# A hybrid decoder trunk on one core: gates by tanh and a new order of gates, roots and stores in the first part of the in-projection

## The chip, the core and the metric

The kernel runs on one core of one Trainium2 chip. The metric is the device time of one execution in microseconds (us), lower is better. The core has a matrix engine (TensorE, PE in the profile; PEld is its weight load), a vector engine (VectorE, DVE), an engine for activation functions (ScalarE, ACT), GpSimd (POOL) and SyncE (SP). SP's queue issues nearly all transfers here, POOL's some that accumulate.

## What is computed

One layer over 1024 positions of width 1024, in float32:

```python
h = rms_norm(x, g_mix)
z = h @ w_in + b_in              # split: conv value, conv gate, rnn, rnn gate, two merge gates
u = va * sigmoid(ga)             # conformer branch, 1024 channels
y = causal_depthwise_conv(u, w[31]) -> layer_norm -> silu -> @ w_a_out
v = causal_depthwise_conv(xb, w[4])                     # RG-LRU branch, 1536 channels
r = sigmoid(block_diag(v, w_rg_a) + b_a)                # 16 heads of 96
i = sigmoid(block_diag(v, w_rg_x) + b_x)
log_a = -8 * r * softplus(-lam);  a = exp(log_a)
mult = sqrt(-expm1(2 * log_a));   mult[0] = 1
h_t = a_t * h_{t-1} + (mult * i * v)_t                  # a scan over positions
y_b = (h * gelu(gb)) @ w_b_out
x = x + (sigmoid(sa) * y_a + sigmoid(sb) * y_b) @ w_o   # y_a: the conformer branch
x = x + relu(rms_norm(x) @ w_1)**2 @ w_2;  final rms_norm
```

(Names are shortened.) The kernel takes sqrt(1 - a^2) as (a + 1) times the square root of tanh of half of -log_a.

## The kernel before

Products in float32 are made of three products of operands split into a high and a low part, so each 128-column chunk of the in-projection takes 24 pairs of weights and activations times two halves of the positions: 48 matmuls of 512 columns (`chunk_mm`, L729).

The program runs in stages: a start to 54 us, the **first part of the in-projection** (a loop over slots s = 3 to 23, one chunk of `w_in` each, to 351 us), the **second part** (products named z, `zseq`, L926, in which seven products of sub-blocks stand for eight, to about 666 us), then the out-projections and the MLP. The change lies in the first part, and in the first steps of the second.

The order of work in a slot is written out by hand, engine by engine. `CH` gives the chunks' order; slot s processes on the other engines the chunk of slot s - 1. A chunk is of one of three kinds: XB (RG-LRU input: `xb_out` makes xb and its width-4 convolution v, three steps of which run on DVE as `rest`, L486; `xb_parts`, L494, splits v into vth and vtl), GA (conformer gate, `u_gate`, L588) or VA (conformer value, `u_out`). Then `w_parts` splits the weights of the next chunk (L65, L67).

Heads: head n begins at slot 4 + n (one later from head 5 on). `head_mm(n, 0)` and `head_mm(n, 1)` are six 96x96 matmuls each (L534 to L536). Both write the one PSUM buffer "ps2", so each waits until `head_gate` (L542) has read the one before. The first product stands at the end of the head's slot, the second in the next slot behind 18 of the chunk's 24 pairs. The gates' results go by SP transfers (L549) from head rows to 128-channel tiles; they have two buffers, tag "g". `head_load` (L511) brings a head's rows of vth and vtl, `head_w` (L515) its weights.

Scan: for each group of four heads (three tiles of 128 channels) `scan_exp` (L558 exponential, L559 tanh) stands at the end of the slot in `EXP` (8, 13, 17, 21), and `scan_root` (L566, square roots) in the slot after it, ahead of `xb_parts` and of the second gate. `scan_in` multiplies the second gate into v, `scan_tile` (L575 to L578) makes the scan, whose store to `hd` is L579. Sigmoid, exponential with tanh, and square root need different activation tables, which ACT_TABLE_LOAD brings.

DVE's work is collected by `later(ready, cost, ...)` and given out by `vector_work`, in order of the time at which a small model of the engines' clocks has it ready. Steps of the width-31 convolution (`conv`, L640, begun by ScalarE at L622 and L623) fill the gaps that the model sees. The convolution's store is to `yd`. In the last slots `x_load` (L670) and `x_sum` make sums of activations (xs) for the second part, `x_parts` (L686) splits them, and `z_load` (L747) brings weights zw.

SP's order in a slot: weight chunk s + 2 (L60), first gate's transfers, second gate's transfers, head weights, xs loads, stores of scan and convolution, inputs of the next head.

Of the kernel before, what the change touches and what calls it, by code (L numbers as in the profile page):

```python
# [15 lines left out]
P = 128  # L16
# [4 lines left out]
HD = 96  # L21
# [9 lines left out]
def trunk_kernel(ctx: ExitStack, tc: tile.TileContext, x, xt_in, xt_eo, vecs, w_in, w_a_out, w_b_out,  # L31
# [107 lines left out]
    cbw_c = vec[:, 344:392]  # L139
    cbb_c = vec[:, 392:404]  # L140
    lam_c = vec[:, 404:416]
    ba_c = vec[0:HD, 416:432]
    bx_c = vec[0:HD, 432:448]

    xt, xc, raw0 = [], [], []

# [118 lines left out]
    c4 = sm[:, 7, :]  # L265
    csum = cp.tile([P, WA // 2, 8], F32, name="csum")
    cab2 = cp.tile([P, 8], F32, name="cab2")

    def decay():
# [53 lines left out]
        ts_(c8, p_, -8.0, None, ALU.mult)  # L323
        yield
        ts_(c4, p_, 4.0, None, ALU.mult)
        yield

    decaying = decay()
# [6 lines left out]
    with tc.manual_schedule(engines={mybir.EngineType.Activation, mybir.EngineType.DVE,  # L335
# [62 lines left out]
                first_z(i, 1, k, "lh")  # L398
        decay()
        nc.vector.tensor_scalar(cab2, cab_c, 2.0, None, ALU.mult)  # L400
        pairs = caw[:, 8:].rearrange("p (i o j) -> p i o j", o=2, j=8)
        nc.vector.tensor_tensor(csum, pairs[:, :, 0, :], pairs[:, :, 1, :], ALU.add)

# [67 lines left out]
    def xb_out(t, ps):  # L471
# [18 lines left out]
        later(ready, 3.8, rest)  # L490

    def xb_parts(t):
        vp_[t] = T(f"vth{t}", F32R), T(f"vtl{t}", F32R)
        nc.scalar.activation(vp_[t][0], vt[t], AF.Copy)  # L494
        h = vp_[t][0].bitcast(F32)
        later(at("A", 1.06), 1.22, nc.vector.tensor_tensor, vp_[t][1], vt[t], h, ALU.subtract)


    gws = {}
# [18 lines left out]
    def head_w_parts(n):  # L518
# [4 lines left out]
        later(at("A", 0.35), 0.35, nc.vector.tensor_tensor, gl, raw, gh.bitcast(F32), ALU.subtract)  # L523
        gws[n] = (gh, gl)

    gps = {}
# [12 lines left out]
    def head_gate(n, gi, ready):  # L539
        g, hh = divmod(n, 4)  # L540
        a = H(f"g{n}_{gi}", "g")
        nc.scalar.activation(a, gps.pop((n, gi))[:HD, :], AF.Sigmoid,  # L542
                             bias=(ba_c, bx_c)[gi][:, n:n + 1])
        at("A", 1.11, ready)
        for (ti, p0, p1, d0) in PIECES[hh]:
            t = 3 * g + ti
            if (gi, t) not in gate:
                gate[gi, t] = T(f"g{gi}_{t}")
            nc.sync.dma_start(gate[gi, t][p0:p1, :], a[d0:d0 + p1 - p0, :])  # L549

    at_, rooted = {}, {}

    def scan_exp(g):
        at("A", 1.28)
        for t in range(3 * g, 3 * g + 3):
            r = gate[0, t]
            at_[t] = T(f"a{t}")
            nc.scalar.activation(at_[t], r, AF.Exp, scale=c8[:, t:t + 1])  # L558
            nc.scalar.activation(r, r, AF.Tanh, scale=c4[:, t:t + 1])  # L559
            at("A", 2.2)  # L560

    def scan_root(g):
        at("A", 2.56)
        for t in range(3 * g, 3 * g + 3):
            r = gate[0, t]
            nc.scalar.activation(r, r, AF.Sqrt)  # L566
            rooted[t] = at("A", 1.06)

    def scan_in(ready, *ts):
        for t in ts:  # L570
            later(ready, 1.2, nc.vector.tensor_tensor, gate[1, t], gate[1, t], vt.pop(t), ALU.mult)

    def scan_tile(t):
        a, r, i = at_.pop(t), gate.pop((0, t)), gate.pop((1, t))
        nc.vector.scalar_tensor_tensor(r, a, 1.0, r, ALU.add, ALU.mult)  # L575
        nc.vector.memset(r[:, 0:1], 1.0)
        nc.vector.tensor_tensor(i, r, i, ALU.mult)
        nc.vector.tensor_tensor_scan(i, a, i, 0.0, ALU.mult, ALU.add)  # L578
        nc.sync.dma_start(hd[t], i)  # L579

    ut = {}
    yd = dp.tile([8, P, S], F32, name="yd")
# [2 lines left out]
    def u_gate(j, ps):  # L585

        ut[j] = u = T(f"u{j}")
        nc.scalar.activation(u.rearrange("p (o n) -> p o n", o=2), ps.rearrange("p (n o) -> p o n", o=2),  # L588
                             AF.Sigmoid, bias=bin_c[:, GA + j:GA + j + 1])
# [15 lines left out]
    def conv(j):  # L605
# [42 lines left out]
        nc.sync.dma_start(yd[j], acc)  # L648
        yield step()
        if j == 0:  # L650
            ysum.append(T("ysum"))
# [20 lines left out]
    def x_sum(c2):  # L672
        q = xq[c2]
        for n, a, b in ((11, 12, 11), (12, 22, 12), (22, 22, 11), (21, 21, 22)):
            later(0, 1.2, nc.vector.tensor_tensor, q[n], q[a], q[b], ALU.subtract)

    def x_parts(c2, *ps):
        for p in ps:
# [5 lines left out]
                at("A", 2.0)  # L684
            else:
                nc.scalar.activation(h, src, AF.Copy)  # L686
                later(at("A", 1.0), 1.2, nc.vector.tensor_tensor, l, src, h.bitcast(F32),
                      ALU.subtract)

    NU = 6  # L690
    CH = [XB, VA, GA, XB + 1, XB + 2, GA + 1, XB + 3, VA + 1, XB + 4, XB + 5, GA + 2]
# [4 lines left out]
    wraw, wst = {}, {}  # L696
    todo, fresh = [], []

    def later(ready, cost, f, *a):

        todo.append((ready, len(todo), cost, f, a))

    def vector_work(end):
        for ready, _, cost, f, a in sorted(todo, key=lambda x: x[:2]):
            dve(cost, ready, f, *a)
        todo.clear()
        taps["wait"] += fresh
        fresh.clear()
        fill(end)

    def w_load(s):
        if s < NC1:
# [87 lines left out]
    HS0 = [4 + n + int(n > 4) for n in range(NH)]  # L800
    head_at = {s: n for n, s in enumerate(HS0)}

    EXP = {head_slot: g for g, head_slot in enumerate(HS0[4 * g + 3] + 1 for g in range(4))}
# [8 lines left out]
    with tc.manual_schedule(engines=ENGINES):  # L812
        for s in range(3, NC1):
            w_load(s + 2)
            taps["hold"] = s > NC1 - 4
            begun = clk["P"]
            clk["A"], clk["V"] = max(clk["A"], begun + 0.5), max(clk["V"], begun - 2)
# [7 lines left out]
                first_parts(rs)  # L825
                chunk_mm(s, 0, 24, (0,))
            else:
                chunk_mm(s, 0, 18)
            before, new, nxt = (head_at.get(s + d) for d in (-1, 0, 1))
            if before is not None:  # L830

                head_gate(before, 0, begun)
                head_mm(before, 1)
            if s > 3:
                chunk_mm(s, 18, 24)
            if new is not None:
                head_mm(new, 0)

# [7 lines left out]
            elif s > 3:  # L846
                u_out(c - VA, zps[s - 1])
            w_parts(s + 1)
            if s - 1 in EXP:

                scan_root(EXP[s - 1])
            if s == 3 or c >= XB:
                vector_work(0)
                xb_parts(0 if s == 3 else c - XB)
            if before is not None:
                head_gate(before, 1, clk["P"] - 12 * MM)
# [6 lines left out]
            for d in range(5):  # L863
                if s - d in EXP:
                    g = EXP[s - d]
                    if d == 0:
                        scan_exp(g)
                        scan_in(begun + 3.5, 3 * g, 3 * g + 1)
                    elif d == 1:
                        scan_in(begun + 3.5, 3 * g + 2)  # L870

                    t = 3 * g + d - 1
                    if 3 * g <= t < 3 * g + 3 and t < 11:
                        later(rooted[t], 4.8, scan_tile, t)
            if s == NC1 - 1:
                z_get(0, z_lhs)
                z_get(1, z_lhs)
# [8 lines left out]
            vector_work(clk["P"] - 0.7)  # L886
            if nxt is not None:
                head_load(nxt)

# [121 lines left out]
    def z_post2(i, p):  # L1011
# [1131 lines left out]
```

## Time and profile before

| what | before |
|---|---|
| median of 3 runs | 1580.93 us (1578.77 to 1581.06) |
| profiled execution | 1581.38 us, span 1579.6 us, mean granted clock 0.989 |
| PE busy | 1538.3 us (97%) |
| DVE busy | 1232.4 us (78%) |
| ACT busy | 918.4 us (58%) |
| POOL busy | 190.4 us (12%) |
| span 0 to 54 us: PE busy, DMA share | 52.28 us, 0.83 |
| span 666 to 1579.6 us: PE busy, DMA share | 905.30 us of 913.6, 0.65 |

Busy times are those of one profiled execution. A row of a timeline gives start, duration, engine, line, operation, what is written and read, and in brackets the idle time before it with what ended it. A matmul's end is modelled, so starts are read rather than ends.

### The profile page before, as it was taken

To read this page: it belongs to the slowest core of one execution; us is meant where nothing else is said; L and a number is where in the kernel's file an instruction comes from. 1 tells how busy PE (TensorE), PEld (TensorE's weight loads), DVE (VectorE), ACT (ScalarE), POOL (GpSimd) and SP (SyncE) were. 2 spreads that over 40 slices of the span, in tenths; PEclk is the share of its full clock that TensorE was granted. 3 is DMA by queue.
4 is the path that set the end of the run, shared out by engine and by line. 5 is a ranking of instruction groups with operands and counts; after the bars stand their busy time and mean duration, and the time that the engine had idled before them with its cause. 6 is when DMAs were issued, how large, how long until landed. Compare 5 with 4: busy or idle time off the path is not lost.

```text
span 1579.6 us, 19214 instructions
## 1 busy us (share of the span) xinstructions
PE 1538.3 (97%) x6758; PEld 1262.7 (80%) x6758; DVE 1232.4 (78%) x1666; ACT 918.4 (58%) x1290; POOL 190.4 (12%) x225
## 2 busy tenths in 40 slices
PE   9997989898999999999999999999999999999998
PEld 7875767686888888888888888888888888888886
DVE  6996678788899999868596978855555558888897
ACT  6747477476666566724447578644444566555553
POOL 0000000011222222100003233000000001111110
PEclk9999989899999999999999999999999999999999
DMA  8785868698997778964469999533333779889862
GB/s 340 204 195 155 206 153 230 179 277 221 235 259 168 166 187 205 283 233 145 137 181 277 240 193 216 167 129 107 107 120 108 214 238 227 214 221 217 214 134 107
DMA packets 133728, 308.35 MB, mean 195 GB/s; under 512 B 13392, under 2 KB 35408, under 8 KB 133632
## 3 DMA queue, kind: packets, MB, share of 16 engines
q1 hardware_dynamic: 102320, 230.60, 44.9%
q0 software_dynamic: 31168, 76.27, 26.5%
q8 instruction: 53, 0.87, 0.2%
q14 instruction: 43, 0.35, 0.1%
q10 hardware_dynamic: 144, 0.26, 0.0%
HBM read 147.69 MB, written 58.72 MB: 131 GB/s over the span
## 4 chain that ended last, share of the span: by engine, by line
PE 84%; DVE 5%; ACT 4%; issue 4%; DMA 2%; POOL 1%; SPq 0%; POOLq 0%; DVEq 0%; ACTq 0%
PE d L1907 14%; PE yb L1140 8%; PE z L729 7%; PE e L2027 3%; PE keep L1907 2%; PE z L258 2%; DVE y L640 1%; ACT g L542 1%; PE rg L534 1%; ACT a L558 1%; DVE yt L640 1%; PE rg L536 1%; DMA vl<-vtl 1%; DVE v L486 1%; PE rg L535 1%
## 5 line engine op out<-in xcount | busy, mean ns | idle before, releaser
L1919 DVE TENSOR_TENSOR acc<-acc,d 128x1024 f32<-128x1024 f32 x72 | 87.8, 1220 | 33.3 <-PE d L1907 32.7
L729 PE MATMUL z<-xh,win_h 128*128 128x512 f32 x336 | 107.4, 397 | 0.0
L729 PE MATMUL z<-xl,win_h 128*128 128x512 f32 x336 | 106.2, 394 | 0.0
L640 DVE SCALAR_TENSOR_TENSOR y<-u,vec,y 128x511 f32<-128x511 f32 (+14 forms) x120 | 88.4, 737 | 9.0 <-ACT y L622 9.0
L542 ACT ACTIVATE g<-rg,vec 96x1024 f32<-96x1024 f32 x32 | 35.6, 1112 | 90.1 <-PE rg L536 51.2
L729 PE MATMUL z<-xh,win_l 128*128 128x512 f32 x336 | 83.0, 391 | 0.0
L640 DVE SCALAR_TENSOR_TENSOR yt<-u,vec,yt 128x511 f32<-128x511 f32 (+6 forms) x112 | 82.6, 737 | 0.0
L640 DVE SCALAR_TENSOR_TENSOR y<-yt,csum,y 128x511 f32<-128x511 f32 (+6 forms) x112 | 82.6, 737 | 0.0
L729 PEld LDWEIGHTS z<-xh,win_h 128*128 128x128 f32 x336 | 64.7, 193 | 15.0 <-ACT win_h L67 0.7
L729 PEld LDWEIGHTS z<-xl,win_h 128*128 128x128 f32 x336 | 64.2, 191 | 13.9
L729 PEld LDWEIGHTS z<-xh,win_l 128*128 128x128 f32 x336 | 63.1, 188 | 14.4
L66 POOL DMA_DIRECT2D zo<-zw x48 | 42.0, 874 | 157.1 <-ACT zo L65 142.4
L1581 ACT ACTIVATE o<-s 128x512 fp32r<-128x512 f32 x56 | 33.8, 624 | 45.7 <-DVE s L1565 26.4
L486 DVE SCALAR_TENSOR_TENSOR v<-xb,vec,v 128x1023 f32<-128x1023 f32 (+2 forms) x36 | 46.2, 1283 | 13.6 <-ACT v L477 12.6
L66 POOL DMA_DIRECT2D win_l<-win_raw x21 | 18.3, 873 | 317.5 <-ACT win_l L65 274.7
L1140 PE MATMUL yb<-hgl,wb_h 128*128 128x512 f32 x168 | 51.7, 389 | 0.0
L1140 PE MATMUL yb<-hgh,wb_h 128*128 128x512 f32 x168 | 51.7, 389 | 0.0
L534 PE MATMUL rg<-vh,rgh 96*96 96x512 f32 x64 | 27.1, 424 | 21.2 <-ACT g L542 15.9
L65 ACT ACTIVATE zo<-zw 128x512 fp32r<-128x512 f32 x48 | 30.0, 625 | 23.6 <-issue 4.2
L66 POOL DMA_DIRECT2D db_1l<-wr x7 | 6.1, 872 | 310.7 <-ACT db_1l L65 288.1
L1140 PE MATMUL yb<-hgh,wb_l 128*128 128x512 f32 x168 | 41.0, 389 | 0.0
L1104 DVE TENSOR_TENSOR o<-s,o 128x512 fp32r<-128x512 f32 x56 | 37.3, 684 | 1.5 <-ACT o L1581 1.4
(1872 smaller groups left out, 4801.3 us busy)
## 6 DMA issues: line engine op xcount, KB each, us to landing
w_raw<-in_w_dram SPq DMA_DIRECT2D x34, 512.0 KB, 5.4
fr<-fd SPq DMA_DIRECT2D x32, 512.0 KB, 5.7
wr<-in_w_dram SPq DMA_DIRECT2D x32, 512.0 KB, 6.5
zw<-in_w_in_dram SPq DMA_DIRECT2D x28, 512.0 KB, 6.2
zo<-zw POOLq DMA_DIRECT2D x48, 256.0 KB, 5.3
win_raw<-in_w_in_dram SPq DMA_DIRECT2D x21, 512.0 KB, 7.7
win_l<-win_raw POOLq DMA_DIRECT2D x21, 512.0 KB, 7.9
zo<-zs POOLq DMA_DIRECT2D x32, 256.0 KB, 6.1
```

Source lines behind the costliest of these rows:

```text
L66: nc.gpsimd.dma_start(l, src, accum_op=ALU.add)
L486: nc.vector.scalar_tensor_tensor(v[:, d:S], a[:, 0:S - d], cbw_c[:, w * 12 + t:w * 12 + t + 1], v[:, d:S], ALU.mult, ALU.add)
L534: nc.tensor.matmul(o, gh[:, gi, :], vh[:, hs], start=True, stop=False)
L542: nc.scalar.activation(a, gps.pop((n, gi))[:HD, :], AF.Sigmoid, bias=(ba_c, bx_c)[gi][:, n:n + 1])
L640: nc.vector.scalar_tensor_tensor(o[:, k:], a[:, 0:HS - k], c, o[:, k:], ALU.mult, add)
L729: nc.tensor.matmul(zps[s][:, HALVES[hf]], w[:, k, :], xw[k][part][hf], start=n == 0, stop=n == 23)
L1104: tt(l, src, h.bitcast(F32), ALU.subtract)
L1140: nc.tensor.matmul(ps[hf], a, b[:, HALVES[hf]], start=n == 0, stop=n == len(todo) - 1)
L1581: nc.scalar.activation(o[:, 0], src, AF.Copy)
L1907: nc.tensor.matmul(o, a, b, start=n == 0 and (p != 1 or g == 0), stop=n == len(todo) - 1, skip_group_check=p == 1 and g > 0)
L1919: tt(acc[p, q2], acc[p, q2], ps, ALU.add)
L2027: nc.tensor.matmul(o, a, b, start=n == 0 and t not in LOADED, stop=n == len(todo) - 1, skip_group_check=t in LOADED)
```

## The change

Seven things are changed together.

- Gates: sigmoid(x) becomes tanh(x / 2), whose factor and summand are folded into what follows: constants of the exponential and tanh (`c8`, `c4`), halved biases (`bhalf`), the root's scale of 0.25, the first column's 0.5, `scan_in` as (gate + 1) * v, and in `u_out` a ScalarE Identity that halves the value in PSUM (one for each of six conformer chunks).
- `scan_exp` of a group's first tile moves one slot earlier; that of the other two stays in the slot of before, behind the second gate.
- `scan_root` moves to the end of its slot, behind the second gate.
- `put` and `flush_puts`: in the first part the second gate's transfers and the stores of scan and convolution are held and issued at the start of the next slot, behind the weight chunk's load. The first gate's transfers are issued at once.
- DVE's work has three ranks (`soon`, `later`, `idle`); `urgent` gives out only rank 0 ahead of `xb_parts`, and the scan's three parts are separate items.
- The second head product stands behind 15 of 24 pairs instead of 18.
- In the second part `x_parts(0, 4)` and `x_parts(1, 4)` move from its steps 0 and 4 to 3 and 5.

```diff
-        nc.scalar.activation(a, gps.pop((n, gi))[:HD, :], AF.Sigmoid,
-                             bias=(ba_c, bx_c)[gi][:, n:n + 1])
+        nc.scalar.activation(a, gps.pop((n, gi))[:HD, :], AF.Tanh, scale=0.5,
+                             bias=bax_h[gi][:, n:n + 1])
...
-            nc.sync.dma_start(gate[gi, t][p0:p1, :], a[d0:d0 + p1 - p0, :])
+            put(gate[gi, t][p0:p1, :], a[d0:d0 + p1 - p0, :], gi == 0)
...
-    def scan_exp(g):
-        at("A", 1.28)
+    def scan_exp(*ts):
+        for t in ts:
+            r = gate[0, t]
+            at_[t] = T(f"a{t}")
+            c = c8[:, t:t + 1], c4[:, t:t + 1]
+            nc.scalar.activation(at_[t], r, AF.Exp, scale=c[0], bias=c[0])
+            nc.scalar.activation(r, r, AF.Tanh, scale=c[1], bias=c[1])
+            at("A", 2.2)
+
+    def scan_root(g):
+        at("A", 1.28)
         for t in range(3 * g, 3 * g + 3):
             r = gate[0, t]
-            at_[t] = T(f"a{t}")
-            nc.scalar.activation(at_[t], r, AF.Exp, scale=c8[:, t:t + 1])
-            nc.scalar.activation(r, r, AF.Tanh, scale=c4[:, t:t + 1])
-            at("A", 2.2)
...
-            nc.scalar.activation(r, r, AF.Sqrt)
+            nc.scalar.activation(r, r, AF.Sqrt, scale=0.25)
             rooted[t] = at("A", 1.06)
+        at("A", 1.28)
...
-            later(ready, 1.2, nc.vector.tensor_tensor, gate[1, t], gate[1, t], vt.pop(t), ALU.mult)
+            idle(ready, 1.28, nc.vector.scalar_tensor_tensor, gate[1, t], gate[1, t], 1.0, vt.pop(t),
+                 ALU.add, ALU.mult)
...
-        later(clk["A"], 1.28, nc.vector.scalar_tensor_tensor, uv,
-              ps.rearrange("p (n o) -> p o n", o=2), bin_c[:, VA + j:VA + j + 1], uv,
-              ALU.add, ALU.mult)
+        nc.scalar.activation(ps, ps, AF.Identity, scale=0.5, bias=bva_h[:, j:j + 1])
+        later(at("A", 1.11), 1.28, nc.vector.scalar_tensor_tensor, uv, uv, 1.0,
+              ps.rearrange("p (n o) -> p o n", o=2), ALU.add, ALU.mult)
...
+    def put(o, i, now=False):
+
+        if now or part[0] > 1:
+            nc.sync.dma_start(o, i)
+        else:
+            held_puts.append((o, i))
...
             w_load(s + 2)
+            flush_puts()
...
-                chunk_mm(s, 0, 18)
+                chunk_mm(s, 0, 15)
...
-            if s - 1 in EXP:
-
-                scan_root(EXP[s - 1])
             if s == 3 or c >= XB:
-                vector_work(0)
+                urgent()
                 xb_parts(0 if s == 3 else c - XB)
...
+            for g, e in EXP.items():
+                if s == e - 1:
+                    scan_exp(3 * g)
+                elif s == e:
+                    scan_exp(3 * g + 1, 3 * g + 2)
+                    scan_in(begun + 3.5, 3 * g, 3 * g + 1)
+                elif s == e + 1:
+                    scan_in(begun + 3.5, 3 * g + 2)
+                    scan_root(g)
+                t = 3 * g + s - e - 1
+                if e < s and t < min(3 * g + 3, 11):
+                    scan_tile(t)
...
-    ZX = {0: ((x_parts, 0, 4), (x_parts, 1, 6)), 1: ((x_parts, 1, 7),), 2: ((x_parts, 1, 5),),
-          4: ((x_parts, 1, 4),), 7: ((later, 0, 4.8, scan_tile, 11),)}
+    ZX = {0: ((x_parts, 1, 6),), 1: ((x_parts, 1, 7),), 2: ((x_parts, 1, 5),),
+          3: ((x_parts, 0, 4),), 5: ((x_parts, 1, 4),), 7: ((scan_tile, 11),)}
```

More of the change, by code (lines that the diff above doesn't have):

```diff
@@ L400, in trunk_kernel @@
         nc.vector.tensor_scalar(cab2, cab_c, 2.0, None, ALU.mult)
+        nc.vector.tensor_scalar(bhalf[:, 0:16], bin_c[:, 0:16], 0.5, None, ALU.mult)
+        nc.vector.tensor_scalar(bhalf[:, 16:48], vec[:, 416:448], 0.5, None, ALU.mult)
         pairs = caw[:, 8:].rearrange("p (i o j) -> p i o j", o=2, j=8)
@@ L488, in rest @@
                                                ALU.mult, ALU.add)
-        later(ready, 3.8, rest)
+        soon(ready, 3.9, rest)
     def xb_parts(t):
@@ L495, in xb_parts @@
         h = vp_[t][0].bitcast(F32)
-        later(at("A", 1.06), 1.22, nc.vector.tensor_tensor, vp_[t][1], vt[t], h, ALU.subtract)
+        soon(at("A", 1.06), 1.22, nc.vector.tensor_tensor, vp_[t][1], vt[t], h, ALU.subtract)
     gws = {}
@@ L522, in head_w_parts @@
         nc.scalar.activation(gh, raw, AF.Copy)
-        later(at("A", 0.35), 0.35, nc.vector.tensor_tensor, gl, raw, gh.bitcast(F32), ALU.subtract)
+        soon(at("A", 0.35), 0.35, nc.vector.tensor_tensor, gl, raw, gh.bitcast(F32), ALU.subtract)
         gws[n] = (gh, gl)
@@ L556, in scan_exp, with start, scan @@
             r = gate[0, t]
-            at_[t] = T(f"a{t}")
-            nc.scalar.activation(at_[t], r, AF.Exp, scale=c8[:, t:t + 1])
-            nc.scalar.activation(r, r, AF.Tanh, scale=c4[:, t:t + 1])
-            at("A", 2.2)
[L562 to L566, printed above, removed]
+            nc.scalar.activation(r, r, AF.Sqrt, scale=0.25)
             rooted[t] = at("A", 1.06)
+        at("A", 1.28)
     def scan_in(ready, *ts):
         for t in ts:
-            later(ready, 1.2, nc.vector.tensor_tensor, gate[1, t], gate[1, t], vt.pop(t), ALU.mult)
+            idle(ready, 1.28, nc.vector.scalar_tensor_tensor, gate[1, t], gate[1, t], 1.0, vt.pop(t),
+                 ALU.add, ALU.mult)
     def scan_tile(t):
         a, r, i = at_.pop(t), gate.pop((0, t)), gate.pop((1, t))
[L575 to L579, printed above, removed]
+        ready = rooted[t]
+        def start():
+            nc.vector.scalar_tensor_tensor(r, a, 1.0, r, ALU.add, ALU.mult)
+            nc.vector.memset(r[:, 0:1], 0.5)
+        def scan():
+            nc.vector.tensor_tensor_scan(i, a, i, 0.0, ALU.mult, ALU.add)
+            put(hd[t], i)
+        idle(ready, 1.35, start)
+        idle(ready, 1.22, nc.vector.tensor_tensor, i, r, i, ALU.mult)
+        idle(ready, 2.3, scan)
     ut = {}
@@ L588, in u_gate @@
         nc.scalar.activation(u.rearrange("p (o n) -> p o n", o=2), ps.rearrange("p (n o) -> p o n", o=2),
-                             AF.Sigmoid, bias=bin_c[:, GA + j:GA + j + 1])
+                             AF.Tanh, scale=0.5, bias=bga_h[:, j:j + 1])
         at("A", 1.11)
@@ L674, in x_sum @@
         for n, a, b in ((11, 12, 11), (12, 22, 12), (22, 22, 11), (21, 21, 22)):
-            later(0, 1.2, nc.vector.tensor_tensor, q[n], q[a], q[b], ALU.subtract)
+            soon(0, 1.2, nc.vector.tensor_tensor, q[n], q[a], q[b], ALU.subtract)
     def x_parts(c2, *ps):
@@ L686, in x_parts @@
                 nc.scalar.activation(h, src, AF.Copy)
-                later(at("A", 1.0), 1.2, nc.vector.tensor_tensor, l, src, h.bitcast(F32),
-                      ALU.subtract)
+                soon(at("A", 1.0), 1.2, nc.vector.tensor_tensor, l, src, h.bitcast(F32),
+                     ALU.subtract)
     NU = 6
@@ L697, in trunk_kernel, with later, soon, idle @@
     todo, fresh = [], []
-    def later(ready, cost, f, *a):
-        todo.append((ready, len(todo), cost, f, a))
+    counter = [0]
+    def later(ready, cost, f, *a, rank=1):
+        counter[0] += 1
+        todo.append((rank, ready, counter[0], cost, f, a))
+    def soon(*a):
+        later(*a, rank=0)
+    def idle(*a):
+        later(*a, rank=2)
+    def work(items):
+        while items:
+            x = min((x for x in items if x[1] <= clk["V"]), default=None) or min(items, key=lambda x: x[1:3])
+            items.remove(x)
+            _, ready, _, cost, f, a = x
+            dve(cost, ready, f, *a)
+    def urgent():
+        first = [x for x in todo if x[0] == 0]
+        todo[:] = [x for x in todo if x[0]]
+        work(first)
     def vector_work(end):
-        for ready, _, cost, f, a in sorted(todo, key=lambda x: x[:2]):
-            dve(cost, ready, f, *a)
+        items = todo[:]
         todo.clear()
+        work(items)
         taps["wait"] += fresh
@@ L709, in vector_work, with flush_puts @@
         fill(end)
+    held_puts = []
+    part = [1]
+    def put(o, i, now=False):
[3 more added lines that the diff above has]
+            held_puts.append((o, i))
+    def flush_puts():
+        for o, i in held_puts:
+            nc.sync.dma_start(o, i)
+        held_puts.clear()
     def w_load(s):
@@ L801, in trunk_kernel @@
     head_at = {s: n for n, s in enumerate(HS0)}
-    EXP = {head_slot: g for g, head_slot in enumerate(HS0[4 * g + 3] + 1 for g in range(4))}
+    EXP = {g: HS0[4 * g + 3] + 1 for g in range(4)}
     XS = {NC1 - 4: ((x_load, 0),), NC1 - 3: ((x_sum, 0),), NC1 - 2: ((x_load, 1), (x_parts, 0, 6)),
@@ L862, in trunk_kernel @@
                 head_w(head_at[s + 2])
[L863 to L874, printed above, removed]
+            for g, e in EXP.items():
[10 more added lines that the diff above has]
+                    scan_tile(t)
             if s == NC1 - 1:
@@ L888, in trunk_kernel @@
                 head_load(nxt)
+        flush_puts()
+        part[0] = 2
     stage.close()
```

15 lines of the change are left out of this document (8 added, 7 removed).

## The prediction

> **What bounds the kernel now.** I read the page first. Its span and busy parts say that TensorE is the bound, and that little of it is free:
>
> ```profile
> span 1579.6 us, 19214 instructions
> PE 1538.3 (97%) x6758; PEld 1262.7 (80%) x6758; DVE 1232.4 (78%) x1666; ACT 918.4 (58%) x1290; POOL 190.4 (12%) x225
> ```
>
> So the question is where the 41 us that PE lacks lie, and at which clock it runs beside them. The windows view, cut by stage, answers that (columns: length, busy us and count of PE, weight loads, DVE, ACT, POOL; granted clock, DMA share, GB/s):
>
> ```profile
> 54.00:66.41 12.41, 12.41 (x55) 10.05 (x56) 11.11 (x13) 8.09 (x10) 1.02 (x2) 1.00 0.94 217
> 66.41:351.06 284.65, 259.36 (x1099) 205.31 (x1098) 223.36 (x286) 177.13 (x180) 17.64 (x21) 0.95 0.77 198
> 351.06:370.42 19.36, 13.42 (x51) 10.33 (x50) 19.28 (x22) 12.12 (x18) 4.14 (x5) 0.91 0.83 204
> 213.60:226.00 12.40, 5.11 (x13) 3.76 (x13) 12.10 (x14) 9.65 (x11) 0.00 (x0) 0.59 0.55 143
> 366.00:660.00 294.00, 293.91 (x1290) 243.24 (x1291) 268.57 (x402) 191.30 (x325) 65.70 (x75) 0.99 0.82 209
> ```
>
> Slots 5 to 23 of the first part (66.41 to 351.06) leave PE idle for 284.65 - 259.36 = 25.3 us at a mean clock of 0.95; the first 19.4 us of the second part leave 5.9 us at 0.91. From there to 660 PE is full at 0.99. The waits view from 60 to 370 us names the waits (total, times, longest):
>
> ```profile
> PE rg L534 <- ACT g L542: 15.9, 4, 7.3
> PE rg L534 <- DMA vh<-vth: 5.3, 1, 5.3
> PE rg L536 <- DMA vl<-vtl: 4.1, 1, 4.1
> PE z0a L926 <- ACT z0b L992: 3.1, 1, 3.1
> PE z1a L926 <- ACT z1b L992: 2.8, 1, 2.8
> ```
>
> The first three are head products. A head's two products share one PSUM buffer, so each waits until ScalarE's gate (L542) has emptied it. The PE timeline shows a slot without a stall and the worst wait:
>
> ```profile
> 172.26 0.40 PE L534 MATMUL rg<-vh,rgh 96*96 96x512 f32 x1
> 172.96 0.39 PE L534 MATMUL rg<-vh,rgh 96*96 96x512 f32 x1
> 186.00 0.40 PE L534 MATMUL rg<-vh,rgh 96*96 96x512 f32 x1
> 220.92 0.74 PE L534 MATMUL rg<-vh,rgh 96*96 96x512 f32 x1 [7.29 <-ACT g L542]
> ```
>
> A slot with two head products takes 186.00 - 172.26 = 13.74 us. Three head matmuls take 172.96 - 172.26 = 0.70, so a product takes 1.40, a slot with one 12.34, one with none 10.94. A chunk's 48 matmuls thus go at 0.228 us each.
>
> What ScalarE did ahead of 220.92 (its timeline in slot 14):
>
> ```profile
> 205.49 1.15 ACT L559 ACTIVATE g<-g,sm 128x1024 f32<-128x1024 f32 x1
> 206.66 1.28 ACT L542 ACT_TABLE_LOAD   x1
> 207.95 1.11 ACT L542 ACTIVATE g<-rg,vec 96x1024 f32<-96x1024 f32 x1
> 208.97 1.10 ACT L474 ACTIVATE xb<-z,vec 128x1024 f32<-128x1024 f32 x1
> 210.10 1.25 ACT L477 ACTIVATE v<-xb,vec 128x1024 f32<-128x1024 f32 x1
> 211.25 1.04 ACT L65 ACTIVATE win_l<-win_raw 128x1024 fp32r<-128x1024 f32 x1
> 212.20 1.04 ACT L67 ACTIVATE win_h<-win_raw 128x1024 fp32r<-128x1024 f32 x1
> 213.25 1.28 ACT L566 ACT_TABLE_LOAD   x1
> 214.54 2.95 ACT L566 ACTIVATE g<-g 128x1024 f32<-128x1024 f32 x3
> 217.40 1.04 ACT L494 ACTIVATE vth<-v 128x1024 fp32r<-128x1024 f32 x1
> 218.46 1.28 ACT L542 ACT_TABLE_LOAD   x1
> 219.75 1.11 ACT L542 ACTIVATE g<-rg,vec 96x1024 f32<-96x1024 f32 x1
> ```
>
> Between the splits and the second gate (219.75) stand two table loads and three square roots: 1.28 + 2.95 + 1.28 = 5.5 us. The first gate too was late, behind six exponential and tanh instructions and a load. The first part has 15 loads, by the view that groups lines:
>
> ```profile
> L542 ACT ACT_TABLE_LOAD x6 | 7.7, 1283 | 0.1
> L558 ACT ACT_TABLE_LOAD x4 | 5.1, 1283 | 0.1
> ```
>
> (the roots' four at L566, of which 213.25 is one, and one at L588 make the 15). The DMA waits come from elsewhere, shown by SyncE's queue:
>
> ```profile
> 131.25 12.34 SPq L549 DMA_DIRECT2D g<-g  x2
> 144.31 0.72 SPq L579 DMA_DIRECT2D hd<-g  x1
> 145.12 0.54 SPq L511 DMA_DIRECT2D vh<-vth  x1
> ```
>
> The second gate's transfers held the queue for 12.34 us until the late gate was there; a store of the scan followed, and only then the inputs of the next head.
>
> **Part 1: table sets, roots and exponentials.** Sigmoid becomes tanh(x/2), with the factors folded into neighbours. Exponential and tanh already run in turn without a load (one load at L558 for six instructions in each of four groups). So the loads in front of the exponentials and of the next gate go, and 4 x 2 remain around the roots: 15 - 8 = 7 loads, 9.0 us of ScalarE. Against that stand six new Identity instructions in `u_out`, at the 1.10 of L474 each: 6.6 us. ScalarE's sum is nearly unchanged; what matters is the order. I walk a slot with time 0 at its chunk's first matmul. PE now: 30 matmuls to 6.8, the second product to 8.2, 18 matmuls to 12.3, the next head's first product to 13.7. The first gate must end by 6.8, the second by 12.3. ScalarE in a value slot: gate 1.1, xb 2.2, v 3.4, two splits 5.5. The three DVE steps of the width-4 convolution follow v:
>
> ```profile
> L486 DVE SCALAR_TENSOR_TENSOR v<-xb,vec,v 128x1023 f32<-128x1023 f32 (+2 forms) x36 | 46.2, 1283 | 13.6 <-ACT v L477 12.6
> ```
>
> 3 x 1.28 = 3.85, so vth runs at 7.3 to 8.4 and the second gate ends at 9.5: 2.8 before it is needed. Of six exponentials and tanhs (1.15 each) two now stand in the slot before and four behind the second gate: they end 14.5, 0.8 into the next slot. That is the root slot: first gate to 1.95, second to 10.4 (slack 1.9), head weights 0.35, load and roots 4.2: 15.1, 1.4 into the next slot. There, load and first gate end at 3.9 against 6.8; slots 15, 19 and 23 work on gate and value chunks of the conformer branch and have no vth, and slot 10 has no gate. No wait is left by this sum. What is late next is the second gate of slots 14 and 18, by 1.9 us of slack.
>
> **Part 2: the queue.** Second gates' transfers and the scan and convolution stores go at the start of the next slot, behind the load of a weight chunk. Head inputs are queued at a slot's end with nothing late ahead; they have some 11 us until use. New is that a scan's store may wait for DVE ahead of the first gate's transfers and the head weights: by the walk in slots 10 and 11, up to 6 us into the slot; the inputs queued behind still have over half a slot. The 5.3 and 4.1 us go.
>
> **Sum for slots 5 to 23.** Ideal: 14 x 13.74 + 3 x 12.34 + 2 x 10.94 = 251.3. Measured 284.65. Gain 33.4, of which 25.3 is idle time and 8.1 slow matmuls behind it: the row 213.60 to 226.00 shows 13 matmul records in 5.1 us at clock 0.59.
>
> **Part 3: the start of the second part.** The rows are of DVE's, ScalarE's and SP's timelines, the fourth of the chain of waits:
>
> ```profile
> 322.06 5.08 DVE L462 TENSOR_TENSOR xs<-xs,xs 128x1024 f32<-128x1024 f32 x4 [9.07 <-issue]
> 364.50 1.06 ACT L686 ACTIVATE xs7h<-xs 128x1024 fp32r<-128x1024 f32 x1 [3.79 <-DVE g L578]
> 366.09 4.49 PE z1a L926 x12
> 315.36 2.04 SPq L670 DMA_DIRECT2D xs<-xu  x4
> ```
>
> DVE stood 9.07 us for xs, whose loads left SP at 315.36, late in the slot, behind a second gate's transfers. From there it ran without a pause, and ScalarE's copies z0b and z1b were late behind it. After the change the loads leave behind the first gate instead, DVE gets those 9 us back, and four `x_parts` subtractions and a scan are ordered behind what z needs first. z0b must end 5.9 us into z and by this sum ends about 2 us earlier. At the pitch of 366 to 660, 293.91 / 1290 = 0.228 us, the 51 matmuls take 11.6 of the 19.36 us: 7.7 gained. The last chain row has the clock's part in it: 12 matmuls in 4.49. [...]
>
> **Costs.** In slot 3 `u_out` stands ahead of the split of the next chunk, for which PE then waits:
>
> ```profile
> 52.86 1.05 ACT L67 ACTIVATE win_h<-win_raw 128x1024 fp32r<-128x1024 f32 x1
> ```
>
> The split ends at 53.91 and the chunk starts at once, so the new Identity costs up to its 1.1 and at least 0: I take 1.0. The other five lie in slots without vth and are covered by 2.7 us and more. Two tiny DVE steps in the start: 0. Residual waits: between 0 and the 9.4 us of DMA waits; I take 2.5, near the low end, since the slack in the walk is never under 1.9. In the second part a move of DVE work (about 4 us of convolution) into a stage where it is busy 268.57 of 294: 25 us of room, 0.
>
> Sum: 33.4 + 7.7 - 1.0 - 2.5 = 37.6. The profiled execution took 1581.38 us (span 1579.6 and 1.8 around it), the median of the runs is 1580.93, 0.45 less: 1580.93 - 37.6 = 1543.3.
>
> **The rivals.** (a) *The start of z keeps its stall*, since DVE's queue into z is full either way: 7.7 back, 1551. For it: DVE has no pause from 322 to 370. Against: the 9.07 us ahead. (b) *Transfers become the bound.* 0.77 x 284.65 = 219 us of DMA time now fits into 254: a share of 0.86. One late head input as at 146 to 157 costs 5.3 + 4.1 and some 2.5 of slow matmuls: 1555. Against: 54.00 to 66.41 ran at a share of 0.94 with PE full. (c) *Other ScalarE waits*: a late DVE uses up the 1.9 us of slack in the root slots, and half of the 15.9 stays, with 2.5 of slow matmuls twice: 1556. Against: DVE is busy 223.36 of 284.65, and the convolution's steps now give way to what is urgent. (d) *The tables still switch at each group*, tanh sharing no set with exp: against it the rows L558 and L559, in turn without loads. The 7 loads would stay on ScalarE, at worst all on the path: 1543 + 9.0 = 1552. (e) *Slower*: held transfers of second gates. Gate outputs have two buffers, so a second gate waits until the last one's transfer, now issued some 2 us into the slot, has landed. From a landing later than 12.3 - 1.1 = 11.2 us into the slot each of 14 slots loses the excess; 37.6 / 14 = 2.7, so from 13.9 on the gain is gone, and at 14.5 it is 1543 + 14 x 3.3 = 1589. The DMA view shows such transfers landing in 4 to 5 us:
>
> ```profile
> g<-g SPq DMA_DIRECT2D x16, 384.0 KB, 4.3
> ```
>
> That puts the landing near 7: unlikely, but queues of the moved stores run before it.
>
> **How the numbers follow.** Forecast (1538 to 1548) 0.60; (a) 0.10; (b) 0.12; (c) 0.07; (d) 0.02; (e) or another loss 0.06; a null 0.03. What a measurement can tell from no change is 0.2%, about 3.2 us. Faster: 0.60 + 0.10 + 0.12 + 0.07 + 0.02 = 0.91. The range goes from 1538 (no residual, no Identity cost, 1543.3 - 3.5 = 1539.8, and 1.8 for the reading of the slot length) to 1558, past (a) to (d).
>
> **What would show it.** Right: table loads in the first part 8; slots of 13.7, 12.3 and 10.9 us throughout, clock 0.98 or more; no PE wait over 1 us on L542's successor; head inputs landing before 9 us into their slot; z's first 51 matmuls in under 13 us. Wrong: waits of rg on the gate with ScalarE idle and a gate buffer's DMA as its releaser (e), on vh (b), of z0a on z0b (a), or on a gate with ScalarE busy (c).

## The result and the profile after

The changed kernel takes 1551.15 us, the median of 5 runs (1550.6 to 1555.04), against 1580.93 us; ratio 0.9819, 95% interval 0.9803 to 0.9835. That is 29.8 us faster. 37.6 us were forecast (1543.3), the range was 1538 to 1558.

The page of the changed kernel, and its waits of PE from 50 to 360 us (total, times, longest):

```profile
span 1553.3 us, 19218 instructions
PE 1532.6 (99%) x6758; PEld 1258.8 (81%) x6758; DVE 1231.3 (79%) x1668; ACT 915.5 (59%) x1289; POOL 190.1 (12%) x225
...
PE rg L537 <- ACT g L545: 5.8, 3, 4.9
PE z1b L975 <- DMA zo<-zs: 2.8, 1, 2.8
PE z L778 <- ACT win_h L67: 1.0, 1, 1.0
PE z0a L975 <- ACT z0b L1041: 1.0, 1, 1.0
```

The profiled execution is the slowest of the five (1555.04 us). A second profile of the same kernel, *again* below, took 1551.85 us, which is nearer to the median. So I read both. The windows view for slots 5 to 23 and for the head of the second part (from its first matmul to the first with xs4, 125 matmuls by the view), first the head of before (its slots stand in the prediction), then of the changed kernel, then of *again*:

```profile
351.06:387.22 36.16, 30.22 (x125) 24.22 (x124) 32.47 (x38) 23.40 (x37) 7.66 (x9) 0.95 0.81 203
```

```profile
67.29:326.56 259.27, 253.46 (x1099) 202.07 (x1098) 225.37 (x286) 175.02 (x181) 19.09 (x22) 0.99 0.85 219
326.56:360.68 34.12, 30.31 (x125) 24.26 (x124) 31.36 (x38) 21.87 (x34) 6.20 (x8) 0.95 0.82 200
```

```profile
67.59:320.91 253.32, 251.81 (x1100) 201.00 (x1098) 224.08 (x285) 173.47 (x178) 18.26 (x21) 1.00 0.86 223
320.91:356.12 35.21, 30.06 (x126) 24.16 (x125) 32.60 (x39) 23.13 (x37) 7.00 (x8) 0.95 0.83 200
```

The slots went from 284.65 to 259.27 us, and to 253.32 in *again*, where the ideal of the prediction was 251.3. The head of the second part went from 36.16 to 34.12 and 35.21: in sum most of its stall is still there, though not in the same place, as is shown below. The slot before (4) ends 0.9 to 1.2 us later. In *again* the account is 31.3 us gained in the slots and 1.0 in the head, less 1.2 at slot 4, 1.1 in the rest of the second part and 0.5 behind it: 29.5, its span being 1550.1.

### The profile page after: what moved, and what is told of

Same layout as the page of the kernel before. It is cut to its first block, busy times and chain, and to the rows that moved or that the text cites. A ratio compares the mean times of both kernels' runs of the same rounds, so it can differ in the third digit from the quotient of the medians.

```text
span 1553.3 us, 19218 instructions
## 1 busy us (share of the span) xinstructions
PE 1532.6 (99%) x6758; PEld 1258.8 (81%) x6758; DVE 1231.3 (79%) x1668; ACT 915.5 (59%) x1289; POOL 190.1 (12%) x225
## 4 chain that ended last, share of the span: by engine, by line
PE 83%; DMA 5%; issue 5%; DVE 4%; POOL 1%; ACT 1%; SPq 0%; POOLq 0%; DVEq 0%; ACTq 0%
PE d L1956 15%; PE z L778 9%; PE yb L1189 8%; PE e L2076 3%; PE keep L1956 2%; DMA g<-g 2%; DMA xs<-xu 1%; PE z L256 1%; PE rg L537 1%; PE rg L538 1%; PE rg L539 1%; DMA x<-in_x_dram 1%; DVE v L489 1%; POOL go L66 1%; DVE g L465 1%
## 5 line engine op out<-in xcount | busy, mean ns | idle before, releaser
L1968 DVE TENSOR_TENSOR acc<-acc,d 128x1024 f32<-128x1024 f32 x72 | 87.8, 1219 | 33.4 <-PE d L1956 32.7
L545 ACT ACTIVATE g<-rg,bhalf 96x1024 f32<-96x1024 f32 x32 | 35.4, 1107 | 51.0 <-PE rg L539 33.1
L66 POOL DMA_DIRECT2D win_l<-win_raw x21 | 18.3, 873 | 289.3 <-ACT win_l L65 225.2
L1189 PEld LDWEIGHTS yb<-hgh,wb_h 128*128 128x128 f32 x168 | 31.5, 188 | 6.6
```

What stands on the lines that cost most here:

```text
L66: nc.gpsimd.dma_start(l, src, accum_op=ALU.add)
L545: nc.scalar.activation(a, gps.pop((n, gi))[:HD, :], AF.Tanh, scale=0.5, bias=bax_h[gi][:, n:n + 1])
L1189: nc.tensor.matmul(ps[hf], a, b[:, HALVES[hf]], start=n == 0, stop=n == len(todo) - 1)
L1968: tt(acc[p, q2], acc[p, q2], ps, ALU.add)
```

## The experiments

The runs fall into four groups: the control, parts of the change taken back, parts put into the kernel before, and other orders at the head of the second part. Times are medians of the timed runs. The kernel before ran at 1580.7 to 1581.6 beside them.

**The control**, the changed kernel itself.

> The changed kernel itself, as a control and for a second profile. The profiled execution on record took 1555.0 us, the median 1551.2. Theory one (the waits of the gate in slot 18 and of z1b for zo both belong to the program): both show again, each within 1 us, and the run is at 1550 to 1555. Theory two (one of them comes and goes with the landing of transfers): one of them is absent in this profile, and the profile's time is nearer 1551.

It took 1551.27 us, ratio 0.9807 (0.9794 to 0.982). Its PE waits:

```profile
PE z1b L975 <- DMA zo<-zs: 2.8, 1, 2.8
PE z0a L975 <- ACT z0b L1041: 2.3, 1, 2.3
PE rg L537 <- ACT g L545: 1.4, 2, 0.9
```

Theory two holds for the gate of slot 18: its 4.9 us wait is absent here. The wait of z1b shows in both. In the profile on record DVE had stood for a tile that a held store of the scan was still reading:

```profile
236.25 1.66 SPq L757 DMA_DIRECT2D hd<-g  x1
...
245.53 1.23 DVE L465 TENSOR_TENSOR vtl<-v,vth 128x1024 fp32r<-128x1024 f32 x1 [6.00 <-DMA hd<-g]
...
259.83 1.06 ACT L497 ACTIVATE vth<-v 128x1024 fp32r<-128x1024 f32 x1 [5.03 <-DVE v L489]
...
261.94 0.67 PE L537 MATMUL rg<-vh,rgh 96*96 96x512 f32 x1 [4.87 <-ACT g L545]
```

The chain is store, tile, DVE (which then works without a pause until the split can start), split, gate, PE. The store landed 9.2 us after its issue, in *again* 5.4. Two other profiles with this order, of *xs4_in_gap* and *scan_behind_sums* below, have the pair again: DVE waits 5.4 and 5.3 us for the store, PE 4.3 and 4.2 us for the gate. What makes the landing differ between executions stays open.

**Stores at once.**

```diff
-            put(hd[t], i)
+            put(hd[t], i, True)
-        put(yd[j], acc)
+        put(yd[j], acc, True)
```

> Only the stores of scan and convolution are issued at once again; second gates' transfers stay held. Theory (a held store keeps a tile from DVE, which stood 6.0 us for vtl's buffer, and the late DVE held the gate of slot 18 for 4.9 us and some 2.4 us of slow matmuls): DVE's wait and PE's wait go, 1544 to 1548 us. Rival (the stores belong behind the head inputs): PE waits for vh or vl, 1553 to 1560 us.

It took 1577.51 us, ratio 0.998 (0.9972 to 0.9989): 26.2 us of the gain were gone. The theory was wrong. The rival had the direction and a small part: PE waited 4.5 us for vh once, in slot 10, which took 18.3 us instead of 12.3. Its gate waits weigh more, 20.4 us in all: slots 15 and 19 took 25.0 and 25.3 us instead of 13.7. Its timelines of SP, then of ScalarE and PE in slot 15, and its waits of ScalarE and of SP:

```profile
215.32 0.33 SPq L751 DMA_DIRECT2D hd<-g  x1
215.74 0.51 SPq L514 DMA_DIRECT2D vh<-vth  x1
...
220.01 1.37 SPq L60 DMA_DIRECT2D win_raw<-in_w_in_dram  x1
221.48 1.79 SPq L757 DMA_DIRECT2D g<-g  x1
```

```profile
230.17 1.11 ACT L545 ACTIVATE g<-rg,bhalf 96x1024 f32<-96x1024 f32 x1 [12.84 <-DMA g<-g]
231.33 0.74 PE L537 MATMUL rg<-vh,rgh 96*96 96x512 f32 x1 [9.83 <-ACT g L545]
```

```profile
ACT g L545 <- DMA g<-g: 38.7, 6, 13.1
SPq L751 <- DVE g L587: 65.0, 6, 15.8
```

The store waits in SP's queue for the scan, which the change has put last on DVE. All behind it waits too, and the held transfer of the second gate leaves only at 221.48. The gate's buffer is free 8.7 us later, and the next second gate stood 12.84 us for it, PE 9.83. This is the mechanism of the prediction's rival (e), the loss through the two gate buffers, with a place and a price. That the stores stand behind the head inputs is what keeps the change from it.

**Second gates at once**, stores held.

```diff
-            put(gate[gi, t][p0:p1, :], a[d0:d0 + p1 - p0, :], gi == 0)
+            put(gate[gi, t][p0:p1, :], a[d0:d0 + p1 - p0, :], True)
```

> Second gates' transfers are issued at once, stores of scan and convolution stay held. Theory (what blocks the queue is a transfer that waits for a late DVE or ScalarE; the second gate now ends near 9.5 us into the slot and is not late): head inputs leave at 10 us instead of earlier, about even, 1549 to 1554 us, and the gates' waits for their own buffers' transfers (11.8 us in the profile of the change) shrink. Rival (holding the second gates is what pays): head inputs late behind them, PE waits for vh, 1560 to 1572 us.

It took 1553.62 us, ratio 0.9829 (0.9815 to 0.9844), within the theory; the interval overlaps the control's. Of the held transfers the stores matter here, the second gates little.

**Roots ahead** of vth and the second gate.

```diff
+            for g, e in EXP.items():
+                if s == e + 1:
+                    scan_root(g)
             if s == 3 or c >= XB:
                 urgent()
...
-                    scan_root(g)
```

> Only the square roots go back ahead of vth and the second gate; tanh gates, spread exponentials and held transfers stay. Theory (the roots' place is the main part of the gain): in a root slot the second gate ends 5.5 us later, 15.9 instead of 10.4 us into the slot against 12.3, so 3.6 us and some 2.4 us of slow matmuls in each of two to four slots: 1563 to 1575 us. Rival (seven table loads fewer and the early exponential give enough room): under 5 us, 1551 to 1556.

It took 1549.9 us, ratio 0.9802 (0.9789 to 0.9816): no loss, as the rival had it, and a little under its span. ScalarE's timeline in slot 14 of this kernel:

```profile
193.60 1.04 ACT L67 ACTIVATE win_h<-win_raw 128x1024 fp32r<-128x1024 f32 x1
194.65 1.28 ACT L569 ACT_TABLE_LOAD   x1
195.94 2.96 ACT L569 ACTIVATE g<-g 128x1024 f32<-128x1024 f32 x3
198.81 1.04 ACT L497 ACTIVATE vth<-v 128x1024 fp32r<-128x1024 f32 x1
```

DVE ends the convolution that vth needs at about 197.5 (three steps in 3.91 us from 193.62). So load and roots fill 2.9 us in which ScalarE would wait anyway, and vth is 1.3 us late, not 5.5. The second gate, behind one more load, starts 12.85 us into this slot, against 12.29 in *again*.

**Sigmoid gates**, and sigmoid with roots ahead. The first undoes the diff's lines on tanh, constants, `scan_in` and the Identity; the second adds the edit above.

> Gates by sigmoid again, with the constants of before and without the six Identity instructions; the order of roots and exponentials, the ranks, the held transfers and the 15 pairs stay. Theory (the queue's order is the main part, table loads only take slack that ScalarE has in most slots): 7 loads of 1.28 us come back, one of them ahead of a first gate and one ahead of exponentials in each group; PE waits for gates by 3 to 8 us in all, 1552 to 1560 us. Rival (the tables are the main part): the gate waits of before, 15.9 us with their slow matmuls, are back: 1570 to 1577 us.

> Sigmoid gates as in sigmoid_back (1555.3 us), and the square roots also back ahead of vth and the second gate; held transfers, ranks, spread exponentials and the 15 pairs stay. Theory (tables and the roots' place back each other up: with tanh only one load stands between roots and second gate, and with roots last the extra loads fall behind the second gate, so each alone is nearly free): both taken away give back gate waits of 3 to 7 us with slow matmuls in two or three slots, 1564 to 1575 us. Rival (the roots' place does not matter at all, as the run with roots ahead and tanh gates says): 1553 to 1558 us.

They took 1555.32 us (ratio 0.984, 0.9826 to 0.9855) and 1557.59 us (0.9852, 0.9839 to 0.9866). The first is within the theory's span: the tables are worth 4.1 us of the time. The count in the theory was off: with the exponentials spread over two slots I count 23 loads in the first part for sigmoid gates, 15 more than the changed kernel's 8 and not 7. That is an estimate from the order of ScalarE's work and the places of the 15 loads of before; it was not shown. For the second the rival's time was right. Its two gate waits of 6.0 and 4.9 us are there as the theory said, and its slots are 6.6 us longer than those of *sigmoid_back*, but PE waits less in the second part. The net is 2.3 us, and the two intervals overlap:

```profile
PE rg L537 <- ACT g L545: 10.9, 2, 6.0
PE z1b L976 <- DMA zo<-zs: 0.8, 1, 0.8
PE z2a L976 <- DMA zo<-zw: 0.7, 1, 0.7
```

**Exponentials in one slot.**

```diff
-                if s == e - 1:
-                    scan_exp(3 * g)
-                elif s == e:
-                    scan_exp(3 * g + 1, 3 * g + 2)
+                if s == e:
+                    scan_exp(3 * g, 3 * g + 1, 3 * g + 2)
```

> The changed kernel with a group's six exponential and tanh instructions in one slot, behind the second gate. Theory (the root slot has 1.9 us of slack by the prediction's walk, and two more instructions take 2.4): waits of 0.5 to 2 us in two or three slots, 1551 to 1556 us. Rival (the spread is a main part): waits of 3 us and more with slow matmuls, 1560 to 1570 us.

It took 1556.32 us, ratio 0.9842 (0.9829 to 0.9856): 5.0 us over the control, 0.3 above the theory's span. Its gate waits are 3.0 and 0.7 us; a wait of 5.4 us for z0b was in neither account. By its profile 5.4 us are lost in the slots against *again* and 2.6 in the head of the second part, and 2.1 come back elsewhere.

**The kernel before with transfers held**, and with roots last as well.

```diff
             w_load(s + 2)
+            flush_puts()
...
-            nc.sync.dma_start(gate[gi, t][p0:p1, :], a[d0:d0 + p1 - p0, :])
+            put(gate[gi, t][p0:p1, :], a[d0:d0 + p1 - p0, :], gi == 0)
...
-        nc.sync.dma_start(hd[t], i)
+        put(hd[t], i)
```

(`yd` likewise, and `put` and `flush_puts` as in the change; in the second kernel `scan_root(g)` moves behind the second gate.)

> The kernel before with one thing of the change: second gates' transfers and the stores of scan and convolution are held to the start of the next slot. Theory (queue order alone removes the waits for vh and vl, 9.4 us with some 2.5 of slow matmuls, and xs comes earlier; the four gate waits of 15.9 us stay): 1564 to 1571 us. Rival (the gate buffers come free later, and gates that are late already get later): no gain or slower, 1578 to 1590 us.

> The kernel before with two things of the change: held transfers and stores (1570.9 us alone), and the square roots behind the second gate. Theory (its two waits of 7.4 and 7.3 us are the roots and loads ahead of the second gate): they go with their slow matmuls, some 2 x 10 us less 2 to 4 that the later first gates lose: 1552 to 1558 us. Rival (loads and roots only move on to the next slot's first gate, and the exponentials in one slot are what is missing): 1564 to 1571 us.

They took 1570.87 us (ratio 0.9943, 0.9927 to 0.996) and 1567.72 us (0.9913, 0.9899 to 0.9926). The queue alone gains 9.8 us, in the theory's span; by its profile 7.5 us come in the slots and 3.1 in the head of the second part. It keeps the gate waits, and one short wait for vl:

```profile
PE rg L534 <- ACT g L542: 18.2, 7, 7.4
...
PE rg L536 <- DMA vl<-vtl: 1.3, 1, 1.3
```

Roots last adds only 3.2 us, the rival's case. Its two long gate waits are 4.0 and 3.9 us in place of 7.4 and 7.3. Its slots gain 5.2 us, and the head gives 2.6 back: z0a waits 5.6 us for z0b.

**Three orders at the head of the second part.** First the two `x_parts` at their old steps, then the scan of tile 10 behind DVE's first sums, then `x_parts(0, 4)` ahead of the split that ScalarE waits for in step 2:

```diff
-    ZX = {0: ((x_parts, 1, 6),), ...  3: ((x_parts, 0, 4),), 5: ((x_parts, 1, 4),), ...
+    ZX = {0: ((x_parts, 0, 4), (x_parts, 1, 6)), ...  4: ((x_parts, 1, 4),), ...
```

```diff
-    def vector_work(end):
-        items = todo[:]
-        todo.clear()
+    def vector_work(end, keep=9):
+        items = [x for x in todo if x[0] < keep]
+        todo[:] = [x for x in todo if x[0] >= keep]
...
-            vector_work(clk["P"] - 0.7)
+            vector_work(clk["P"] - 0.7, 2 if s == NC1 - 1 else 9)
```

(The last slot leaves DVE's work of the lowest rank to the next call.)

```diff
-          3: ((x_parts, 0, 4),), 5: ((x_parts, 1, 4),), 7: ((scan_tile, 11),)}
+          5: ((x_parts, 1, 4),), 7: ((scan_tile, 11),)}
...
             z_get(n - 2, z_post2)
+            if n == 2:
+                x_parts(0, 4)
```

> Only x_parts(0, 4) and x_parts(1, 4) go back to steps 0 and 4 of the second part. Theory (the moved split puts ScalarE work and a 512 KB transfer ahead of the transfer of zo for which z1b waited 2.8 us, with 2.1 us of slow matmuls): that wait goes, 1546 to 1548 us. Rival (DVE's tail ahead of z sets these waits, and the split at step 0 delays z0b): the wait of z0a for z0b grows from 1.0 to 3 us or more, 1550 to 1554 us.

> The changed kernel, but the scan of tile 10 stands behind the first sums of the second part's weights on DVE. Theory (DVE's queue into the second part sets the wait of z0a for z0b, 1.0 and 2.3 us in two profiles): sums come 1.2 to 1.9 us earlier, that wait goes, z1b's wait for zo shrinks by as much or stays: 1547 to 1549.5 us. Rival (transfers set both): no change, 1550 to 1552 us.

> The changed kernel with x_parts(0, 4) of the second part moved from its step 3 into step 2, ahead of the split that ScalarE waits for there (3.4 us idle, for DVE's sums). Theory (the two ScalarE instructions of 2.1 us and the 512 KB transfer ahead of zo's transfer make z1b wait 2.8 us and then run at a low clock): that wait goes, 1546 to 1549 us. Rival (DVE's late sums or the transfers' share set it wherever the split stands): z1b or a neighbour waits as long, 1550 to 1553 us.

The first took 1551.21 us (ratio 0.9806, 0.9792 to 0.9819), as its rival said. z1b's wait goes, and z0a waits longer:

```profile
PE z0a L975 <- ACT z0b L1041: 4.3, 1, 4.3
PE z0a L975 <- DMA zo<-zw: 1.6, 1, 1.6
```

The second took 1553.6 us (ratio 0.9841, 0.9817 to 0.9864): neither case. z0a still waited 1.5 us, and z1b's wait for zo grew to 4.1; but the execution that was profiled took 1561.28 us, and the others need not have waited so. The third took 1549.15 us (ratio 0.9798, 0.9784 to 0.9813), between the spans of theory and rival. Its interval overlaps the control's, so the timing does not show a gain; the trace does show that the head of the second part has no stall left:

```profile
326.23:354.34 28.11, 28.11 (x125) 23.20 (x124) 27.87 (x35) 20.68 (x32) 5.26 (x6) 1.00 0.90 219
```

All 28.11 us are busy. Against the profile on record, which has slot 18's wait as this one has, the head is 6.0 us shorter, and 1.3 us come back as a later wait of z2a for zo. Its second part begins 5.3 us later than that of *again*, which gives DVE more time ahead of it. A kernel that has both this head and slots as short as those of *again* was not run.

## Why the prediction was right, and where it was not

**Bound and direction: right.** PE was the bound and its waits in the slots were recoverable: 31.3 of the 33.4 us in *again*, 25.4 in the profile on record, where slot 18's wait takes 4.9 us and its slow matmuls 1.7 more (ten in 3.95 us from 261.94 on, against 2.28 at 0.228 each). With the allowance of 2.5 us for residual waits 30.9 were forecast, which lies between. The clock in the slots rose from 0.95 to 0.99 and 1.00, and slots without a wait take 13.73, 12.34 and 10.88 us, as said.

**The queue: right in size, incomplete in reason.** 9.4 us of waits for head inputs with their slow matmuls were to go; held transfers alone gained 9.8, though 3.1 of it in the head of the second part, and in the slots the waits for gates grew by 2.3. That the same order also carries the rest, because late scans ahead of head inputs and second gates would cost 26 us, was not seen in part 2. The mechanism stood among the rivals as (e); I had placed it in the change, and it strikes the version that lacks one part of it.

**Tables and roots: the size of ScalarE's sum was right, the reading of the order was not.** Loads fell to 8 as said: groups of the changed kernel (the row is the roots' four; three at L545 and one at L601 make 8):

```profile
L569 ACT ACT_TABLE_LOAD x4 | 5.1, 1283 | 0.1
```

I read the 5.5 us of roots and loads ahead of the second gate as time on its path, and put the gain on "the order". In the changed kernel the roots ahead cost nothing, tables 4.1 us, exponentials in one slot 5.0. The walk had the number that should have told: ScalarE waits from 5.5 to 7.3 us for DVE in each value slot, and a part of the roots fits there. Its slack of 1.9 us in the root slots was not there either: it has the second gate end 10.4 us into the slot, in slot 14 of *again* it ended at 13.4, and PE waited 0.9 us.

Along one path of kernels the gain splits as follows (median; then slots 5 to 23 and the head of the second part, by the starts of matmuls in each profile):

| kernel | us | slots | head |
|---|---|---|---|
| before | 1580.93 | 284.65 | 36.16 |
| *before_held* | 1570.87 | 277.17 | 33.11 |
| *sigmoid_roots_ahead* | 1557.59 | 266.40 | 29.21 |
| *sigmoid_back* (roots last) | 1555.32 | 259.80 | 31.57 |
| *again* (tanh) | 1551.27 | 253.32 | 35.21 |

The second step, 13.3 us, is what *sigmoid_roots_ahead* has beside held transfers (spread exponentials, DVE's ranks, the 15 pairs, the smaller moves). It is not taken apart further: ranks and pairs were not tried by themselves. Roots last and tanh gain 6.6 and 6.5 us in the slots, of which 2.3 and 4.1 are left in the time, the first with intervals that overlap: much of it goes into waits at the head. Over the last three rows the second part begins 11.9 us earlier, but DVE's first sum for it (zs) only 7.8.

**The start of the second part: the old stall went in good part, and a new one came.** Of the 7.7 us forecast, 1.0 to 2.0 came. What is missing, 5.7 to 6.7, is most of the 7.9 us by which the forecast was too fast; in *again* another 1.6 us were lost behind the head, where I had put 0. The prediction's own window, the first 51 matmuls, did shorten, from 19.36 us to 12.65, and to 13.95 in *again* (under 13 was said). The windows are of the changed kernel, of *again*, and of *z_parts_as_before*:

```profile
326.56:339.21 12.65, 11.63 (x51) 9.31 (x50) 12.62 (x14) 6.28 (x10) 1.81 (x3) 1.00 0.96 224
```

```profile
320.91:334.86 13.95, 11.65 (x51) 9.30 (x50) 13.89 (x15) 7.58 (x13) 2.61 (x3) 1.00 0.97 221
```

```profile
320.01:339.42 19.41, 13.54 (x51) 10.36 (x50) 18.18 (x20) 15.21 (x21) 4.35 (x5) 0.91 0.95 209
```

The rest of the head then takes 21.47 and 21.26 us instead of 16.80. There z1b waits for zo, whose transfer stands behind that of xs4 in POOL's queue. In *again* (POOL, then PE):

```profile
340.20 0.87 POOL L66 DMA_DIRECT2D xs4l<-xs  x1 [11.77 <-ACT xs4l L65]
341.94 0.87 POOL L66 DMA_DIRECT2D zo<-zs  x1 [0.87 <-ACT zo L65]
```

```profile
349.43 1.22 PE L975 MATMUL z1b<-xs6h,zo 128*128 128x512 f32 x2 [2.85 <-DMA zo<-zs]
```

So the first step that failed is the move of `x_parts(0, 4)` to step 3, which I had costed nowhere: with its slow matmuls the new wait costs 4.7 and 4.5 us. *z_parts_as_before* has the split at its old step, the whole old stall and no wait of z1b; *xs4_in_gap* has it in step 2 and neither stall. The time is that of rival (a), which had 0.10, but (a) has the old stall kept: that its number came out is luck.

The second step that failed left z0a's wait of 1.0 and 2.3 us. z0b began 6.45 us into the second part, 2.1 earlier than the 8.53 of before, but in *again* 7.73. DVE did not get "those 9 us back": in *again* it stood 3.05 us for the held transfer of a second gate and 3.8 us for xs, ran scans among its sums, and the sums were late for ScalarE's split that stands ahead of z0b (DVE, then ScalarE):

```profile
309.60 1.23 DVE L465 SCALAR_TENSOR_TENSOR g<-g,v 128x1024 f32<-128x1024 f32 x1 [3.05 <-DMA g<-g]
326.63 0.63 ACT L65 ACTIVATE zo<-zs 128x512 fp32r<-128x512 f32 x1 [3.01 <-DVE zs L465]
```

**Slot 4: right.** 1.0 us was taken for the Identity ahead of the split; PE waited 1.0 for win_h.

**Transfers as the bound (b): no.** The share in the slots rose from 0.77 to 0.85 and 0.86, and no head input was late.

## What to carry to other kernels

In SP's queue here an entry that waits holds up all that stands behind it (in *stores_at_once* stores waited for their scans up to 15.8 us each): when work is moved later on one engine, move its stores behind everything that does not need them. Before an instruction's time is counted as delay, look whether its engine was to wait at that place anyway; here 2.9 of the 4.2 us of three roots and a load lay in such a wait. When a stage ahead gets shorter, the next stage's preparations must get shorter too, and their order is worth a walk of its own.

## What the runs showed of the hardware

No one length of PE's gaps divides those with slow matmuls behind them from those without. In PE's timelines of the fourteen profiles between 54 and 400 us, gaps of up to 2.30 us (in *again*) were followed by matmuls at 0.23 us, and all from 3.86 us on (in *before_held_roots_last*) by some at 0.43. Between these two lengths both happen. Slow ones followed gaps of 2.38 (*roots_ahead*), 2.44 (*stores_at_once*), 2.65 (*sigmoid_back*), 2.79 (the changed kernel), 2.85 (before and *again*) and 3.03 us (*exponentials_in_one_slot*); after 2.60 (*second_gate_at_once*) and 3.10 us (before) they went on at 0.23. Two of these, of *sigmoid_back* and of before:

```profile
204.75 0.55 PE L537 MATMUL rg<-vh,rgh 96*96 96x512 f32 x1 [2.65 <-ACT g L545]
205.10 0.63 PE L538 MATMUL rg<-vh,rgl 96*96 96x512 f32 x1
205.53 0.63 PE L539 MATMUL rg<-vl,rgh 96*96 96x512 f32 x1
...
208.09 0.77 PE L777 MATMUL z<-xl,win_h 128*128 128x512 f32 x2
208.70 0.63 PE L777 MATMUL z<-xh,win_h 128*128 128x512 f32 x2
```

```profile
360.21 0.50 PE L926 MATMUL z0a<-xh,zo 128*128 128x512 f32 x1 [3.10 <-ACT z0b L992]
360.55 0.40 PE L926 MATMUL z0a<-xl,zo 128*128 128x512 f32 x1
360.78 0.63 PE L926 MATMUL z0a<-xh,zo 128*128 128x512 f32 x2
```

In the first case ten matmuls take the 3.95 us from 204.75 to 208.70, against 2.28 at 0.228 each, which is 1.7 us beyond the gap; over all gaps with slow matmuls behind them in these timelines the cost was 1.5 to 3.2 us. In the prediction's row of clock 0.91 (351.06 to 370.42) the gap of 3.10 us left the matmuls at 0.23, and the one of 2.85 us behind it was followed by eight in 3.41 us, against 1.82 at 0.228 each.
